# Mixing the tiles of the first feed-forward product among the seven products of the second in a fixed order, with the squares on the scalar engine

## The chip, the core and the metric

The kernel runs on one core of a Trainium2 chip. The metric is the device time of one launch in microseconds (us), less is better. Three runs of the kernel before gave 1634.02, 1637.30 and 1638.63 us.

## What is computed

A trunk of two layers over 512 latent tokens and 256 context tokens with 1024 features. Each layer has a group of mixers, an output projection, and then a squared-ReLU feed-forward block (4096 hidden features) with a gated residual and a layer norm. Layer 1 no longer needs the context's feed-forward. All of it is float32. What matters here:

```python
def channel_mlp(h, w1, w2):
    return jnp.square(jax.nn.relu(h @ w1)) @ w2
...
        f = channel_mlp(modulate(x, m[3], m[4]), w_ff1[l], w_ff2[l])
        x = layer_norm_affine(DN_ALPHA * x + m[5] * f, ln2_g[l], ln2_b[l])
```

In layer 0 the context goes through the same block with its own modulation and its own gate.

## The kernel before

**Products.** TensorE multiplies at reduced precision, so each float32 operand is split into a high half (a rounded copy, by the scalar engine) and a low half (the rest, a subtraction on the vector engine), and one product is three matmuls (`mm3`, line 135). A weight tile is a raw load into the pool `raw` of four rotating buffers (`pr`), then its two halves in the pool `W` (`load_w`, line 154; scalar engine line 162, vector engine line 165).

**The feed-forward block** is `ffn` (line 1181), called once per layer by `run`. N is 768 tokens in layer 0 (latent and context) and 512 in layer 1. The 4096 hidden features are 32 feature tiles of 128, f0 to f31, in eight chunks of four. A feature tile is 16 (layer 0: for latent and context separately) or 8 steps of three matmuls: 48 matmuls in layer 0, half of them 512 and half 256 columns wide, and 24 of 512 columns in layer 1. A relu (line 1199) takes it out of PSUM.

The second product of a chunk, squares of four feature tiles times 512 rows of w2, is done by the Strassen-Winograd scheme: tokens are halved (`half`), features are taken in pairs of tiles (two pairs per chunk), outputs are halved, and seven products with sums and differences of the blocks replace eight. Each product has HT row tiles (3 in layer 0, 2 in layer 1), and for each 6 matmuls of 512 columns: 18 or 12 matmuls per product. The parts:

- `operands` (line 1256): squares on GpSimd (line 1262), four sums per pair on GpSimd (line 1281), halves by the scalar engine (line 1274) and vector engine (line 1275), into tiles `fop`.
- `weights` (line 1295): four raw loads of w2, halves (lines 1307 and 1308), four differences on GpSimd (line 1312), which are written over the raw tiles.
- `ff2_chunk` (line 1327): the seven products; each result is added from PSUM into accumulators `acc` or the shared part `base` by the vector engine (line 1338). Between two products `more()` asks for the next operands.

The loop runs over chunks 0 to 6. A chunk's turn first builds the four feature tiles of the chunk after it (`ff1`), then its own seven products; the order on TensorE is left to the scheduler. The first chunk's tiles come from `ff1_first`, ahead of the loop. The last chunk, f28 to f31, has no Strassen products: its tiles are squared by `square` (line 1201) and go through an ordinary second product, `ff2_tile` (line 1373), 12 or 8 units of 12 matmuls behind everything else.

**The tail.** The gate rows are broadcast to 128 partitions by `rows2(0)` ahead of the loop (`bcast_rows`, line 1434: a DMA issued by the scalar engine in program order). Behind the loop each 128-row accumulator gets the shared part (vector engine, line 1418), is multiplied by the gate (GpSimd, line 1419) and gets the residual row `rawx` (vector engine, line 1420), which was loaded through the same four `raw` buffers (line 1414). Then come the rows ln2g and ln2b (`rows2(1)`), the four w2 tiles of the tail (`ff2_w`, line 1364), also through `raw`, the units with the gate applied (`fft`, line 1385, then an addition on GpSimd, line 1386), and the layer norm of each row tile.

Small pools that matter: `G`, four buffers (tag G), which hold `base`, the gates and the norm rows; PSUM: PA with three single banks, PF with one, P2 with two double banks.

Of the kernel before, what the change touches and what calls it, by code (L numbers as in the profile page):

```python
# [9 lines left out]
F32 = mybir.dt.float32  # L10
F32R = mybir.dt.float32r
AF = mybir.ActivationFunctionType
ALU = mybir.AluOpType
# [5 lines left out]
NL = 512  # L19
NC = 256  # L20
# [27 lines left out]
class Trunk:  # L48
# [102 lines left out]
                out=lo, in0=src, scalar=scale, in1=hi.bitcast(F32), op0=ALU.mult, op1=ALU.subtract  # L151
            )

    def load_w(self, pieces, shape, name, gate=None):

        nc = self.nc
        raw = self.pr.tile(shape, F32, name=self.nm("raw" + name), tag="raw")
        for sl, src in pieces:
            self.load(out=raw[sl], in_=src)
        hi = self.pw.tile(shape, F32R, name=self.nm("hi" + name), tag="W")  # L160
        lo = self.pw.tile(shape, F32R, name=self.nm("lo" + name), tag="W")
        i = nc.scalar.activation(out=hi, in_=raw, func=AF.Copy)  # L162
# [279 lines left out]
    def proj_T(self, l, hL, hC, c0, nf, evict, ctx_too, name):  # L442
# [738 lines left out]
    def ffn(self, l, hL, hC, x, xc, rows2, mod2, done):  # L1181
        nc, A = self.nc, self.A
        w1 = A["w_ff1"][l].rearrange("(k p) n -> p k n", p=128)
        w2 = A["w_ff2"][l].rearrange("(f p) n -> p f n", p=128)
        NCH = DFF // 512
        full = hC is not None

        def ff1_w(f):
            W = self.load_w([((slice(None),), w1[:, :, 128 * f:128 * f + 128])], [128, 8, 128], "w1",
                            self.gate if f < 8 else None)  # L1190
# [17 lines left out]
        N = NL + NC if full else NL  # L1208
        half = N // 2
        HT = half // 128  # L1210

        def ff1(c):
            rs = []
            for f in range(4 * c, 4 * c + 4):
                W = ff1_w(f)
                ps = self.P2("ff1")
                ff1_mm(ps[:, :NL], hL, 0, W)
                if full:
                    ff1_mm(ps[:, NL:NL + NC], hC, 0, W)
                r = self.T("relu", 768)  # L1220
                relu(r, 0, ps[:, :N])
                rs.append(r)
            return rs

        def ff1_first():

# [26 lines left out]
                            relu(rs[f - 1 + i], NL, big[:, 512 * i:512 * i + 256])  # L1253
            return rs

        def operands(rs):

            pool = nc.gpsimd  # L1260
            for r in rs:
                pool.tensor_tensor(out=r[:, :N], in0=r[:, :N], in1=r[:, :N], op=ALU.mult)  # L1262
            q = []
            for p in range(2):
                tmp = self.T("fsum", 768)
                e, o = rs[2 * p], rs[2 * p + 1]
                q.append((e[:, :half], o[:, :half], e[:, half:N], o[:, half:N], tmp[:, :half], tmp[:, half:N]))

            def halves(k):
                res = []  # L1270
                for v in q:
                    z = self.Z("fop")
                    hi, lo = z[:, :half], z[:, half:N]
                    nc.scalar.activation(out=hi, in_=v[k], func=AF.Copy)  # L1274
                    nc.vector.tensor_tensor(out=lo, in0=v[k], in1=hi.bitcast(F32), op=ALU.subtract)  # L1275
                    res.append((hi, lo))
                return res

            def sums(o, a, b, op):
                for v in q:  # L1280
                    pool.tensor_tensor(out=v[o], in0=v[a], in1=v[b], op=op)

            yield halves(0)
            sums(4, 2, 3, ALU.add)
            yield halves(4)
            sums(5, 4, 0, ALU.subtract)
            yield halves(5)
            sums(4, 1, 5, ALU.subtract)
            yield halves(4)
            sums(2, 0, 2, ALU.subtract)  # L1290
            yield halves(2)
            yield halves(1)
            yield halves(3)

        def weights(c):

            pool = nc.gpsimd
# [12 lines left out]

            def diff(o, a, b):
                pool.tensor_tensor(out=o, in0=a, in1=b, op=ALU.subtract)  # L1312

            b11, b12, b22, b21 = raw(0, 0), raw(0, 1), raw(1, 1), raw(1, 0)
            yield halves(b11)
            diff(b11, b12, b11)
            yield halves(b11)
            diff(b11, b22, b11)
            yield halves(b11)
            diff(b12, b22, b12)  # L1320
            yield halves(b22)
            yield halves(b12)
            yield halves(b21)
            diff(b21, b21, b11)
            yield halves(b21)

        def ff2_chunk(c, left, acc, base, more):


            B = weights(c)  # L1330
            seen = set()

            def add(ps, key, sl):
                if c == 0 and key not in seen:
                    seen.add(key)
                    nc.scalar.activation(out=sl, in_=ps, func=AF.Copy)
                else:
                    nc.vector.tensor_tensor(out=sl, in0=ps, in1=sl, op=ALU.add)  # L1338

            for i, to in enumerate((("11", "B"), ("12", "22"), ("B",), ("12",), ("21", "22"), ("11",), ("21",))):  # L1340
                if i % 2 == 0:
                    banks = [self.PA("ff2") for _ in range(HT)]
                else:
                    big = self.P2("ff2")
                    banks = [big[:, 0:512], big[:, 512:1024]]
                    if HT > 2:
                        banks.append(self.PF("ff2") if i == 3 else self.P2("ff2")[:, 0:512])
                W, a = next(B), left[i]
                for t in range(HT):
                    for p in range(2):  # L1350
                        self.mm3(
                            banks[t], [h[:, 128 * t:128 * t + 128] for h in a[p]],
                            [h[:, p, :] for h in W], p == 0, p == 1,
                        )
                    for q in to:
                        if q == "B":
                            sl = base[t]
                        else:
                            n = int(q[1]) - 1
                            sl = acc[HT * (int(q[0]) - 1) + t][:, 512 * n:512 * n + 512]  # L1360
                        add(banks[t], (q, t), sl)
                more()

        def ff2_w(c, n):
            return [
# [22 lines left out]
        rs = ff1_first()  # L1388
        big = [self.G([128, 1024], "base") for _ in range((HT + 1) // 2)]
        base = [big[t // 2][:, 512 * (t % 2):512 * (t % 2) + 512] for t in range(HT)]  # L1390
        gl, gc = rows2(0)

        xr = self.pd.tile([N, D], F32, name=self.nm("xr"), tag=self.nm("xr"))
        for j, t in enumerate(x + (xc or [])):
            nc.sync.dma_start(out=xr[128 * j:128 * j + 128, :], in_=t)
        acc = [self.X([128, 1024], "acc") for _ in range(N // 128)]
        left = list(operands(rs))
        for c in range(NCH - 1):
            nxt, ops = [], None
            if c < NCH - 2:  # L1400
                ops = operands(ff1(c + 1))
                nxt += [next(ops), next(ops)]

            def more():
                if ops is not None:
                    nxt.extend([z for z in [next(ops, None)] if z is not None])

            ff2_chunk(c, left, acc, base, more)
# [256 lines left out]
```

## Time and profile before

| what | us |
|---|---|
| median of three runs | 1637.3 |
| lowest, highest | 1634.02, 1638.63 |
| profiled execution, its own time | 1640.47 |
| span of its trace | 1638.4 |
| TensorE busy | 1484.5 (91%) |
| vector engine busy | 1102.6 (67%) |
| scalar engine busy | 661.7 (40%) |
| GpSimd busy | 600.9 (37%) |

The profile is of one execution. PE is TensorE's matmul, PEld its weight load, DVE the vector engine, ACT the scalar engine, POOL is GpSimd, SP issues most loads; ACTq and SPq are DMA issues. Times in the views are us from the start of the span. PEclk is the mean granted clock of TensorE, 1.00 for 2.4 GHz and 0.50 for 1.2 GHz.

### The profile page before, as it was taken

To read this page: it belongs to the slowest core of one execution; us is meant where nothing else is said; L and a number is where in the kernel's file an instruction comes from. 1 tells how busy PE (TensorE), PEld (TensorE's weight loads), DVE (VectorE), ACT (ScalarE), POOL (GpSimd) and SP (SyncE) were. 2 spreads that over 40 slices of the span, in tenths; PEclk is the share of its full clock that TensorE was granted. 3 is DMA by queue.
4 is the path that set the end of the run, shared out by engine and by line. 5 is a ranking of instruction groups with operands and counts; after the bars stand their busy time and mean duration, and the time that the engine had idled before them with its cause. 6 is when DMAs were issued, how large, how long until landed. Compare 5 with 4: busy or idle time off the path is not lost. (4 is left out here: it accounts for less than half of the span.)

```text
span 1638.4 us, 23881 instructions
## 1 busy us (share of the span) xinstructions
PE 1484.5 (91%) x9228; PEld 1226.5 (75%) x9228; DVE 1102.6 (67%) x1811; ACT 661.7 (40%) x1207; POOL 600.9 (37%) x478
## 2 busy tenths in 40 slices
PE   5899889999999899999997989989989999898895
PEld 3689667787988687787876767867778778777674
DVE  3384655566574847648399589575465877678896
ACT  3433455425562323323221355355436643334331
POOL 1021333233363252432525151143242655443633
PEclk9999899999999999999999889999998999999997
DMA  8442366265212302123014423245265122233152
GB/s 287 142 117 63 122 217 193 80 223 179 78 39 65 98 29 80 39 64 91 28 62 128 130 78 116 65 149 162 86 217 179 52 89 91 81 100 103 52 154 77
DMA packets 150954, 180.45 MB, mean 110 GB/s; under 512 B 9096, under 2 KB 96568, under 8 KB 150840
## 3 DMA queue, kind: packets, MB, share of 16 engines
q1 hardware_dynamic: 140792, 160.42, 31.3%
q10 hardware_dynamic: 10048, 18.49, 3.4%
q8 instruction: 73, 1.20, 0.3%
q14 instruction: 41, 0.34, 0.1%
HBM read 169.43 MB, written 9.46 MB: 109 GB/s over the span
## 5 line engine op out<-in xcount | busy, mean ns | idle before, releaser
L133 PE MATMUL ff<-hiw,fop 128*128 128x512 f32 x980 | 325.0, 406 | 36.3 <-DVE acc L1338 35.6
L133 PEld LDWEIGHTS ff<-hiw,fop 128*128 128x128 f32 x980 | 191.3, 195 | 87.9 <-DVE acc L1338 25.3
L133 PE MATMUL ff<-hh,hiw 128*128 128x512 f32 (+1 forms) x672 | 241.6, 360 | 13.6 <-DVE acc L1338 9.5
L1308 DVE TENSOR_TENSOR low<-raww,hiw 128x1024 fp32r<-128x1024 f32 x98 | 136.7, 1397 | 159.7 <-ACT hiw L1307 159.4
L133 PE MATMUL ff<-hl,hiw 128*128 128x512 f32 (+1 forms) x672 | 240.4, 358 | 0.0
L133 PE MATMUL ff<-hh,low 128*128 128x512 f32 (+1 forms) x672 | 239.4, 356 | 0.7 <-DVE low L165 0.7
L1262 POOL TENSOR_TENSOR relu<-relu 128x768 f32<-128x768 f32 (+1 forms) x56 | 91.2, 1631 | 318.3 <-ACT relu L1199 318.3
L133 PE MATMUL ff<-low,fop 128*128 128x512 f32 x490 | 199.2, 406 | 6.7 <-DVE low L1308 6.7
L1307 ACT ACTIVATE hiw<-raww 128x1024 fp32r<-128x1024 f32 x98 | 103.2, 1060 | 231.6 <-PE ff L133 157.7
L1338 DVE TENSOR_TENSOR acc<-ff,acc 128x512 f32<-128x512 f32 x260 | 167.9, 676 | 12.3 <-PE ff L133 12.2
L1312 POOL TENSOR_TENSOR raww<-raww,raww 128x1024 f32<-128x1024 f32 x56 | 137.3, 2452 | 86.7 <-DVE low L1308 67.5
L133 PEld LDWEIGHTS ff<-hh,hiw 128*128 128x128 f32 x672 | 128.8, 192 | 36.0 <-issue 13.6
L133 PEld LDWEIGHTS ff<-hh,low 128*128 128x128 f32 x672 | 128.0, 190 | 19.2 <-DVE low L165 1.1
L133 PEld LDWEIGHTS ff<-hl,hiw 128*128 128x128 f32 x672 | 128.8, 192 | 18.0
L162 ACT ACTIVATE hiw<-raww 128x1024 fp32r<-128x1024 f32 x64 | 66.5, 1057 | 143.0 <-PE ff L133 103.2
L133 PEld LDWEIGHTS ff<-low,fop 128*128 128x128 f32 x490 | 95.5, 195 | 32.1 <-DVE low L1308 13.0
L547 POOL TENSOR_SCALAR p<-p,rec 128x768 f32<-128x768 f32 (+3 forms) x80 | 63.4, 796 | 143.1 <-DVE rec L546 133.4
L1275 DVE TENSOR_TENSOR fop<-relu,fop 128x384 fp32r<-128x384 f32 (+1 forms) x112 | 87.0, 801 | 39.9 <-ACT fop L1274 39.9
L165 DVE TENSOR_TENSOR low<-raww,hiw 128x1024 fp32r<-128x1024 f32 x64 | 82.0, 1289 | 14.6 <-ACT hiw L162 14.5
L133 PE MATMUL ada<-wada,sc 128*32 128x128 f32 x1536 | 62.4, 300 | 22.5 <-DMA wada<-in_w_ada 22.5
L1275 DVE TENSOR_TENSOR fop<-fsum,fop 128x384 fp32r<-128x384 f32 (+1 forms) x84 | 75.0, 914 | 7.3 <-ACT fop L1274 7.3
L1274 ACT ACTIVATE fop<-relu 128x384 fp32r<-128x384 f32 (+1 forms) x112 | 50.2, 466 | 68.1 <-POOL relu L1262 34.3
(362 smaller groups left out, 3237.7 us busy)
## 6 DMA issues: line engine op xcount, KB each, us to landing
raww<-in_w_ff SPq DMA_DIRECT2D x120, 512.0 KB, 4.2
wada<-in_w_ada SPq DMA_DIRECT2D x96, 512.0 KB, 4.6
rawwo<-in_w_out SPq DMA_DIRECT2D x16, 512.0 KB, 7.7
rawx<-xr SPq DMA_DIRECT2D x10, 512.0 KB, 3.4
rawz<-in_w_ff SPq DMA_DIRECT2D x8, 512.0 KB, 4.6
xr<-x SPq DMA_DIRECT2D x8, 512.0 KB, 5.1
rawwb<-in_w_in SPq DMA_DIRECT2D x12, 256.0 KB, 4.3
gate<-grow ACTq DMA_DIRECT2D x6, 512.0 KB, 7.2
```

The source lines that it names most:

```text
L133: return self.pinned(self.nc.tensor.matmul(out, lhsT, rhs, start=start, stop=stop))
L162: i = nc.scalar.activation(out=hi, in_=raw, func=AF.Copy)
L165: nc.vector.tensor_tensor(out=lo, in0=raw, in1=hi.bitcast(F32), op=ALU.subtract)
L547: nc.gpsimd.tensor_scalar(out=p[:, :keep], in0=p[:, :keep], scalar1=rec, scalar2=1.0, op0=ALU.mult, op1=ALU.mult)
L1262: pool.tensor_tensor(out=r[:, :N], in0=r[:, :N], in1=r[:, :N], op=ALU.mult)
L1274: nc.scalar.activation(out=hi, in_=v[k], func=AF.Copy)
L1275: nc.vector.tensor_tensor(out=lo, in0=v[k], in1=hi.bitcast(F32), op=ALU.subtract)
L1307: nc.scalar.activation(out=hi, in_=t, func=AF.Copy)
L1308: nc.vector.tensor_tensor(out=lo, in0=t, in1=hi.bitcast(F32), op=ALU.subtract)
L1312: pool.tensor_tensor(out=o, in0=a, in1=b, op=ALU.subtract)
L1338: nc.vector.tensor_tensor(out=sl, in0=ps, in1=sl, op=ALU.add)
```

## The change

Four things, all in `ffn`:

1. TensorE's instructions are chained in the order of the program within the loop (`self.pin = True`; `mm` then makes each matmul follow the one before), and that order is a string per chunk: f is a feature tile of the chunk after, a digit a product. "f01f23f45f6" for chunks 0 to 5, "01f23f456ff" for chunk 6, whose four tiles are f28 to f31.
2. Operands are made per pair, as soon as its two tiles are there; their squares are done by the scalar engine. The products come in another order with other targets, the differences of weights are rearranged accordingly (four per chunk, as before), and the accumulators' first writes (copies by the scalar engine) are kept over chunks in `seen`.
3. The raw loads of w1 within the loop go through the pool `G` (`spare=True`) instead of `raw`.
4. The gate rows, `rows2(0)`, are loaded behind the loop.

```diff
-    def load_w(self, pieces, shape, name, gate=None):
+    def load_w(self, pieces, shape, name, gate=None, spare=False):
...
-        raw = self.pr.tile(shape, F32, name=self.nm("raw" + name), tag="raw")
+        raw = self.G(shape, "raw" + name) if spare else self.pr.tile(
+            shape, F32, name=self.nm("raw" + name), tag="raw")
...
-        def operands(rs):
+        def operands(e, o):
...
-            for r in rs:
-                pool.tensor_tensor(out=r[:, :N], in0=r[:, :N], in1=r[:, :N], op=ALU.mult)
+            for r in (e, o):
+                nc.scalar.activation(out=r[:, :N], in_=r[:, :N], func=AF.Square)
+            tmp = self.T("fsum", 768)
+            a11, a12, a21, a22 = e[:, :half], o[:, :half], e[:, half:N], o[:, half:N]
+            s1, s2 = tmp[:, :half], tmp[:, half:N]
...
+            z11 = halves(a11)
+            pool.tensor_tensor(out=s1, in0=a21, in1=a22, op=ALU.add)
+            pool.tensor_tensor(out=s2, in0=s1, in1=a11, op=ALU.subtract)
+            pool.tensor_tensor(out=a21, in0=a11, in1=a21, op=ALU.subtract)
+            pool.tensor_tensor(out=a11, in0=a12, in1=s2, op=ALU.subtract)
+            return [z11] + [halves(v) for v in (a11, a12, s1, s2, a21, a22)]
...
-            b11, b12, b22, b21 = raw(0, 0), raw(0, 1), raw(1, 1), raw(1, 0)
+            b11, b22, b21, b12 = raw(0, 0), raw(1, 1), raw(1, 0), raw(0, 1)
             yield halves(b11)
...
+            diff(b12, b12, b11)
+            yield halves(b22)
+            diff(b22, b22, b12)
             diff(b11, b22, b11)
...
+            diff(b21, b21, b22)
+            for t in (b12, b22, b11, b21):
+                yield halves(t)
+
+        TO = (("11", "B"), ("12",), ("11",), ("12", "22"), ("B",), ("21", "22"), ("21",))
+
+        def product(i, B, left, acc, base, seen):
...
-        gl, gc = rows2(0)
...
-        left = list(operands(rs))
+        left = [operands(rs[2 * p], rs[2 * p + 1]) for p in range(2)]
+        seen = set()
+        self.pin = True
         for c in range(NCH - 1):
-            nxt, ops = [], None
-            if c < NCH - 2:
-                ops = operands(ff1(c + 1))
-                nxt += [next(ops), next(ops)]
...
+            B = weights(c)
+            rs, nxt = [], []
+            order = "f01f23f45f6" if c < NCH - 2 else "01f23f456ff"
+            for o in order:
+                if o != "f":
+                    product(int(o), B, left, acc, base, seen)
+                    continue
+                rs.append(ff1_tile(4 * c + 4 + len(rs), True))
+                if c < NCH - 2 and len(rs) % 2 == 0:
+                    nxt.append(operands(*rs[-2:]))
             left = nxt
-
-        rs = ff1(NCH - 1)
+        self.pin = None
+
+        gl, gc = rows2(0)
```

TensorE in a chunk of layer 0, before. Each row is the first matmul of a group with one output; `ff` tiles fed by `hh` are feature tiles (48 matmuls each), those fed by `fop` are row tiles of products.

```order
L133 MATMUL ff_1249_5934<-hiw_1251_5936,fop_5393 128x512
...
L133 MATMUL ff_1261_5996<-hh_4127,hiw_1259_5992 128x512
...
L133 MATMUL ff_1266_6053<-hh_4127,hiw_1264_6049 128x512
...
L133 MATMUL ff_1271_6110<-hh_4127,hiw_1269_6106 128x512
...
L133 MATMUL ff_1276_6167<-hh_4127,hiw_1274_6163 128x512
...
L133 MATMUL ff_1284_6238<-hiw_1291_6249,fop_5726 128x512
...
L133 MATMUL ff_1295_6285<-hiw_1297_6288,fop_5734 128x512
...
L133 MATMUL ff_1309_6362<-hiw_1310_6364,fop_5820 128x512
```

The same place now:

```order
L133 MATMUL ff_1259_5992<-hh_4127,hiw_1257_5988 128x512
...
L133 MATMUL ff_1261_6043<-hiw_1268_6054,fop_5672 128x512
...
L133 MATMUL ff_1270_6082<-hiw_1272_6085,fop_5679 128x512
...
L133 MATMUL ff_1277_6116<-hh_4127,hiw_1275_6112 128x512
...
L133 MATMUL ff_1287_6195<-hiw_1290_6200,fop_5682 128x512
...
L133 MATMUL ff_1292_6225<-hiw_1294_6228,fop_5685 128x512
...
L133 MATMUL ff_1299_6262<-hh_4127,hiw_1297_6258 128x512
...
L133 MATMUL ff_1301_6313<-hiw_1304_6316,fop_5688 128x512
```

Four feature tiles stood together, then all seven products; now a tile, two products, a tile, two products, and so on.

GpSimd in a chunk of layer 1 now; rows of `raww` are weight differences, rows of `fsum` and `relu` are the operand sums (the second output into `relu` is the left operand of product 1):

```order
L1295 TENSOR_TENSOR raww_2671_13315<-raww_2671_13315,raww_2668_13309 128x1024
L1274 TENSOR_TENSOR fsum_13228<-relu_13150,relu_13224 128x256
L1295 TENSOR_TENSOR raww_2669_13311<-raww_2669_13311,raww_2671_13315 128x1024
L1275 TENSOR_TENSOR fsum_13228<-fsum_13228,relu_13150 128x256
L1276 TENSOR_TENSOR relu_13150<-relu_13150 128x256
L1295 TENSOR_TENSOR raww_2668_13309<-raww_2669_13311,raww_2668_13309 128x1024
L1277 TENSOR_TENSOR relu_13150<-relu_13224,fsum_13228 128x256
L1295 TENSOR_TENSOR raww_2670_13313<-raww_2670_13313,raww_2669_13311 128x1024
```

The sums of one pair and the four weight differences stand in turn; the squares that stood here are gone.

The scalar engine at the end of layer 0's loop now (`gate` are the moved loads):

```order
L1204 ACTIVATE fh_8471<-relu_8361 128x768
L1200 ACTIVATE relu_8418<-ff_1598_8369 128x768
L1416 DMA gate_8420<-grow_4403 128x1024
L1416 DMA gate_8422<-grow_4405 128x1024
L1416 DMA ln2g_8457<-in_ln_g 128x1024
L1416 DMA ln2b_8459<-in_ln_b 128x1024
L1204 ACTIVATE fh_8476<-relu_8418 128x768
L163 ACTIVATE hiw_1619_8483<-raww_1618_8481 128x1024
```

Before, the two gate loads stood among the first relus ahead of the loop, and only ln2g and ln2b here. SP still has the six `rawx` loads ahead of the tail's four weight loads.

## Rows read from the trace of the kernel before

**Rows 1.** Busy time of each engine over the whole execution (page, part 1).

```profile
PE 1484.5 (91%) x9228; PEld 1226.5 (75%) x9228; DVE 1102.6 (67%) x1811; ACT 661.7 (40%) x1207; POOL 600.9 (37%) x478
```

**Rows 2.** Busy time by stretch: layer 0's loop, its tiles, its products.

```profile
core 0: us, PE busy (x) PEld busy (x) DVE busy (x) ACT busy (x) POOL busy (x), PEclk, DMA share, GB/s
436.76:921.42 484.66, 453.39 (x2229) 378.29 (x2228) 327.26 (x390) 153.64 (x221) 200.71 (x117) 0.97 0.23 68
638.14:671.55 33.41, 33.41 (x192) 29.59 (x193) 8.32 (x7) 6.81 (x9) 15.88 (x9) 1.00 0.10 32
671.55:706.79 35.24, 31.49 (x129) 24.49 (x127) 34.06 (x49) 14.02 (x21) 10.38 (x7) 0.95 0.32 90
```

**Rows 3.** The same, layer 1's loop, its first two tiles, a steady chunk.

```profile
1266.13:1595.66 329.53, 303.53 (x1263) 242.65 (x1262) 262.37 (x316) 134.81 (x212) 171.51 (x113) 0.96 0.30 92
1266.13:1277.04 10.91, 10.91 (x51) 9.02 (x49) 6.90 (x7) 5.66 (x15) 9.67 (x10) 1.00 0.24 88
1418.27:1465.31 47.04, 42.97 (x182) 34.69 (x181) 35.90 (x45) 19.10 (x30) 23.49 (x17) 0.96 0.29 90
```

**Rows 4.** Waits of TensorE in 430 to 870 us (total, times, longest).

```profile
PE ff L133 <- DVE acc L1338: 18.3, 23, 2.1
```

**Rows 5.** Waits of TensorE in 1290 to 1600 us.

```profile
PE ff L133 <- DVE acc L1338: 21.2, 9, 3.7
```

**Rows 6.** Timeline, layer 1's loop end: start, us, engine, line, operation.

```profile
1580.73 1.21 DVE L1420 TENSOR_TENSOR acc<-acc,rawx 128x1024 f32<-128x1024 f32 x1
...
1587.25 1.06 ACT L162 ACTIVATE hiw<-raww 128x1024 fp32r<-128x1024 f32 x1 [6.61 <-DMA raww<-in_w_ff]
1588.21 0.58 ACT L1199 ACTIVATE relu<-ff 128x512 f32<-128x512 f32 x1
1588.83 0.63 ACT L1203 ACTIVATE fh<-relu 128x512 fp32r<-128x512 f32 x1
...
1591.07 1.22 DVE L165 TENSOR_TENSOR low<-raww,hiw 128x1024 fp32r<-128x1024 f32 x1
```

**Rows 7.** GpSimd by line in 1418.27 to 1465.31: busy us, mean ns, idle before.

```profile
L1312 POOL TENSOR_TENSOR raww<-raww,raww 128x1024 f32<-128x1024 f32 x5 | 12.1, 2418 | 3.5 <-DVE low L1308 3.4
L1262 POOL TENSOR_TENSOR relu<-relu 128x512 f32<-128x512 f32 x4 | 6.3, 1564 | 18.5 <-ACT relu L1199 18.5
L1281 POOL TENSOR_TENSOR relu<-relu 128x256 f32<-128x256 f32 x2 | 2.6, 1318 | 0.0
...
L1281 POOL TENSOR_TENSOR fsum<-relu,relu 128x256 f32<-128x256 f32 x2 | 1.5, 734 | 0.1
```

**Rows 8.** Timeline of the scalar engine: issues of the row broadcasts.

```profile
327.43 1.21 ACTq L1437 DMA_DIRECT2D gate<-grow  x2
...
437.02 0.33 ACTq L1437 DMA_DIRECT2D gate<-grow  x1
...
921.47 0.34 ACTq L1437 DMA_DIRECT2D ln2g<-in_ln_g  x1
```

**Rows 9.** Timeline of GpSimd, multiplications by the gate, layer 0.

```profile
879.20 9.44 POOL L1419 TENSOR_TENSOR acc<-acc,gate 128x1024 f32<-128x1024 f32 x3 [5.89 <-DVE acc L1338]
889.27 6.12 POOL L1419 TENSOR_TENSOR acc<-acc,gate 128x1024 f32<-128x1024 f32 x2 [0.62 <-DVE acc L1418]
```

**Rows 10.** Timeline of the vector engine, residual additions, layer 0.

```profile
889.72 9.03 DVE L1420 TENSOR_TENSOR acc<-acc,rawx 128x1024 f32<-128x1024 f32 x4
```

**Rows 11.** Timeline of SP's issues, layer 0's loop end.

```profile
869.87 23.61 SPq L116 DMA_DIRECT2D rawx<-xr  x6
896.50 6.47 SPq L116 DMA_DIRECT2D raww<-in_w_ff  x4
```

**Rows 12.** The gate tiles' loads, all six.

```profile
DMA to landing us min/median/max: 4.1/7.2/10.2
```

**Rows 13.** Busy time by stretch, the tails (columns as in rows 2).

```profile
921.42:958.93 37.51, 34.86 (x145) 27.70 (x143) 29.57 (x49) 9.60 (x18) 18.75 (x15) 0.95 0.28 91
1595.66:1623.41 27.75, 25.69 (x96) 19.39 (x95) 19.17 (x32) 6.68 (x10) 11.41 (x10) 0.88 0.19 64
```

More of the change, by code (lines that the diff above doesn't have):

```diff
@@ L1186, in ffn, with ff1_w @@
         full = hC is not None
-        def ff1_w(f):
+        def ff1_w(f, spare=False):
             W = self.load_w([((slice(None),), w1[:, :, 128 * f:128 * f + 128])], [128, 8, 128], "w1",
-                            self.gate if f < 8 else None)
+                            self.gate if f < 8 else None, spare)
             return [[W[j][:, k, :] for j in range(2)] for k in range(KT)]
@@ L1210, in ffn, with ff1_tile @@
         HT = half // 128
[L1212 to L1223, printed above, removed]
+        def ff1_tile(f, spare):
+            W = ff1_w(f, spare)
+            ps = self.P2("ff1")
+            ff1_mm(ps[:, :NL], hL, 0, W)
+            if full:
+                ff1_mm(ps[:, NL:NL + NC], hC, 0, W)
+            r = self.T("relu", 768)
+            relu(r, 0, ps[:, :N])
+            return r
         def ff1_first():
@@ L1254, in ff1_first @@
             return rs
-        def operands(rs):
+        def operands(e, o):
             pool = nc.gpsimd
-            for r in rs:
-                pool.tensor_tensor(out=r[:, :N], in0=r[:, :N], in1=r[:, :N], op=ALU.mult)
[L1263 to L1293, printed above, removed]
@@ new lines, in operands, with halves @@
+            for r in (e, o):
[3 more added lines that the diff above has]
+            s1, s2 = tmp[:, :half], tmp[:, half:N]
+            def halves(v):
+                z = self.Z("fop")
+                hi, lo = z[:, :half], z[:, half:N]
+                nc.scalar.activation(out=hi, in_=v, func=AF.Copy)
+                nc.vector.tensor_tensor(out=lo, in0=v, in1=hi.bitcast(F32), op=ALU.subtract)
+                return hi, lo
@@ L1295, in weights @@
+            z11 = halves(a11)
[4 more added lines that the diff above has]
+            return [z11] + [halves(v) for v in (a11, a12, s1, s2, a21, a22)]
         def weights(c):
-            pool = nc.gpsimd
             def raw(odd, n):
@@ L1311, in diff @@
             def diff(o, a, b):
-                pool.tensor_tensor(out=o, in0=a, in1=b, op=ALU.subtract)
-            b11, b12, b22, b21 = raw(0, 0), raw(0, 1), raw(1, 1), raw(1, 0)
+                nc.gpsimd.tensor_tensor(out=o, in0=a, in1=b, op=ALU.subtract)
+            b11, b22, b21, b12 = raw(0, 0), raw(1, 1), raw(1, 0), raw(0, 1)
             yield halves(b11)
-            diff(b11, b12, b11)
-            yield halves(b11)
+            diff(b12, b12, b11)
+            yield halves(b22)
+            diff(b22, b22, b12)
@@ L1318, in weights @@
             diff(b11, b22, b11)
[L1319 to L1322, printed above, removed]
             yield halves(b21)
[L1324 to L1362, printed above, removed]
@@ new lines, in weights @@
+            diff(b21, b21, b22)
[3 more added lines that the diff above has]
+        def product(i, B, left, acc, base, seen):
+            if i in (0, 2, 4, 6):
+                banks = [self.PA("ff2") for _ in range(HT)]
+            else:
+                big = self.P2("ff2")
+                banks = [big[:, 0:512], big[:, 512:1024]]
+                if HT > 2:
+                    banks.append(self.PF("ff2"))
+            W = next(B)
+            for t in range(HT):
+                ps = banks[t]
+                for p in range(2):
+                    self.mm3(
+                        ps, [h[:, 128 * t:128 * t + 128] for h in left[p][i]],
+                        [h[:, p, :] for h in W], p == 0, p == 1,
+                    )
+                for q in TO[i]:
+                    if q == "B":
+                        sl = base[t]
+                    else:
+                        n = int(q[1]) - 1
+                        sl = acc[HT * (int(q[0]) - 1) + t][:, 512 * n:512 * n + 512]
+                    if (q, t) in seen:
+                        nc.vector.tensor_tensor(out=sl, in0=ps, in1=sl, op=ALU.add)
+                    else:
+                        seen.add((q, t))
+                        nc.scalar.activation(out=sl, in_=ps, func=AF.Copy)
@@ L1396, in ffn @@
         acc = [self.X([128, 1024], "acc") for _ in range(N // 128)]
-        left = list(operands(rs))
+        left = [operands(rs[2 * p], rs[2 * p + 1]) for p in range(2)]
+        seen = set()
+        self.pin = True
         for c in range(NCH - 1):
-            nxt, ops = [], None
-            if c < NCH - 2:
-                ops = operands(ff1(c + 1))
-                nxt += [next(ops), next(ops)]
[L1404 to L1408, printed above, removed]
+            B = weights(c)
[8 more added lines that the diff above has]
+                    nxt.append(operands(*rs[-2:]))
             left = nxt
-        rs = ff1(NCH - 1)
+        self.pin = None
+        gl, gc = rows2(0)
         for j, t in enumerate(acc):
```

## The prediction

> **What bounds the kernel now.** I read the page's busy table first: TensorE is busy 91% of the span [rows 1], so a reordering can only win what TensorE loses in gaps and at the lower clock. The view of stretches then shows where it loses. In layer 0 the loop runs from the first tile behind the opening to the end of the last feature tile, 484.66 us, with TensorE busy 453.39 and a mean granted clock of 0.97 [rows 2]. Its four feature tiles of one chunk take 33.41 us for 192 matmuls with no gap at all; the seven products behind them take 35.24 us with 31.49 busy and a clock of 0.95 [rows 2]. In layer 1 the loop takes 329.53 us with 303.53 busy, a steady chunk 47.04 with 42.97 [rows 3].
>
> What would the loops take without loss? In layer 1 the first two tiles, 48 matmuls of 512 columns, take 10.91 us at full clock [rows 3] (the row counts 51 records that touch the stretch), so one takes 10.91/48 = 0.2273 us. A chunk of layer 0 is 33.41 us of tiles and 7 x 18 = 126 product matmuls, 28.64 us: 62.05, and seven of them 434.3. The loop takes 484.66, so **50.3 us are lost**. A chunk of layer 1 is 96 + 84 matmuls, 40.91 us, seven 286.4, of 329.53: **43.1 us lost**. Together 93.4.
>
> The view of waits names the loss: in 430 to 870 us TensorE's product matmuls wait 18.3 us in 23 waits for the vector engine's evictions (line 1338) [rows 4]; in layer 1 21.2 us in 9 waits for the evictions, up to 3.7 at once [rows 5]. The rest of the 93 is clock: 0.95 over 35.24 us costs 1.76 us per chunk, and the clock falls in the stretch with the waits, not in the tiles. The reason is in the vector engine's load: it is busy 8.32 of the 33.41 us of tiles and 34.06 of the 35.24 us of products [rows 2]. It idles through one half and is full in the other. Over a whole chunk it is not full: in layer 1 35.90 of 47.04 us [rows 3]. Averaged over a chunk without gaps that is 35.90/40.91 = 88%.
>
> **The change part by part.**
>
> *The mixed order.* All matmuls stay; now no more than two products stand between two tiles (before: seven together). A layer-0 pair of products (2 x 18 matmuls, 8.2 us) is followed by a tile (33.41/4 = 8.35 us), in which its evictions can finish. So the vector engine's 88% in layer 1, and less in layer 0 (42.39 us by the row of tiles plus products, 8.32 + 34.06, of 62.05, 68%), is spread evenly, and most of the 93.4 us goes. What is late next is the operand chain of product 1. Its left operand for the second pair needs the last tile's relu, square, four sums on GpSimd (the fourth is the operand), a copy and a low half. From that tile's end until product 1 TensorE has product 6, a tile and product 0. In layer 1 that is 12 + 24 + 12 = 48 matmuls, 10.9 us. The chain is 0.58 + 0.63 (relu and square, [rows 6]), 4 sums of 0.73 to 1.32, about 4.0 [rows 7], some 1.1 for copy and low half: 6.7, and with the two weight differences of 2.42 [rows 7] that stand among the sums in the new GpSimd order 11.6. So it is 4 us early if the differences pass before it, 0.7 late if both fall in it. In layer 0 the time is 18 + 18 matmuls and a tile, 16.5 us, and the sums are longer by half, about 13.5 with both differences: no wait. I keep a residue of 0.5 us per chunk in layer 0 (4 in all) and 1.1 in layer 1 (8 in all; waits of 0.7 with some clock). Its bounds are 0, and 3.5 per chunk, where the whole gain is gone (below). **Loops: 93.4 - 12 = -81 us.**
>
> *Squares on the scalar engine.* 56 of 1.6 to 1.8 us leave GpSimd [rows 7]. On ScalarE the nearest row is the tail's square, 0.63 us for 512 columns [rows 6], four per chunk: 2.5 us on an engine that is busy 19.10 of 47.04 [rows 3]. That costs nothing as long as it stays half idle; without this cover it would be those 2.5 us a chunk. GpSimd's 6.3 us per chunk go, which is what brings the chain above to 11.6 rather than later.
>
> *First-product weights through another pool; operands per pair; targets and weight order changed.* Same bytes and the same instructions, but for the squares; nothing on the path.
>
> *The gate loads behind the loop.* This is the cost. Before, the two gate broadcasts of layer 0 were issued from 437.02 us on [rows 8] and had landed long before use: by the end of the last tile (E, 921.42) the last multiplications by the gate (889.27 + 6.12) and most residual additions (four in 889.72 + 9.03) were done [rows 9, 10], and so the weights of the last second-product tiles, which rotate through the same four buffers as the six residual rows, were issued from 896.50 on [rows 11]. Now the scalar engine issues the gates only after the last relu; the ln2g load in the same place of the old program went out at 921.47, E + 0.05 [rows 8]. A gate takes 4.1 us to land at best, 7.2 in the median, 10.2 at worst [rows 12]; with nothing else loading I take 4.1. Then, in layer 0: three multiplications at 9.44/3 = 3.15 [rows 9], the third residual addition 1.21 [rows 6], which frees the buffer that the first of the four weight loads needs. From the end of such an addition to the start of the weight's first half was 1587.25 - (1580.73 + 1.21) = 5.3 us in layer 1, where the load waited for just that; half 1.06, low half 1.22 [rows 6]. Sum: E + 0.05 + 4.1 + 9.45 + 1.21 + 5.3 + 1.06 + 1.22 = **E + 22.4**. Each further weight tile follows a further multiplication, 3.15 apart: the fourth at E + 31.8. Behind it stand ten of the twelve units, 27 to 31 us (5/6 of the tail's 34.86 busy us [rows 13] is 29), so TensorE ends at E + 62 to 66, where it was 37.5 [rows 13]: +24 to +28, **I take 26**. In layer 1 there are only four residual rows for four buffers, so the first weight waits for the first addition alone: E + 0.05 + 4.1 + 3.15 + 1.21 + 5.3 + 2.28 = E + 16.1, the fourth at E + 25.5, six of eight units behind it (3/4 of 25.69 is 19.3): E + 44 to 48 against 27.75 [rows 13]: **+18**. Bounds for both tails: 38 (first values of both ranges, units overlapping better) and 56 (TensorE has idled, so the restart runs partly at the lower of the two levels, 1.2 instead of 2.4 GHz: the tail of layer 1 ran at 0.88 after its small gaps [rows 13], 12% of 50 us is 6, twice).
>
> The Trainium skill, page "DMA: Bandwidth & Descriptors", section "Rules for kernel authors", says to issue a load early and to wait late; this part of the change does the opposite, and the rows above are its price, 44 us against none.
>
> *Sum:* 1640.5 (the profiled execution) - 81 + 44 = 1603. The profiled execution stands 3.2 us above the median of the runs, so by the median **1600 us**. Its own range, with the residue from 0 to 1.8 per chunk in both layers and the tails from 38 to 56: 1582 to 1625.
>
> **Rivals.**
>
> *The operand chain takes the place of the eviction wait (slower).* Before product 1 TensorE waits in every chunk, since the weight differences on GpSimd themselves wait (3.4 us for the low half that reads the same buffer [rows 7]) and hold the sums behind them, in order. One difference and one sum are 2.42 + 0.74 = 3.2 us of wait, and the clock takes 1.76 more as it does now: 5 us per chunk, 70 over fourteen. The gain is then 23 and the tails cost 44: +21, **1658**. It decides from (93.4 - 44)/14 = 3.5 us per chunk. For it: the vector engine's 88% and the order of GpSimd. Against it: 3 to 4 us of slack in layer 0. Chance 0.12.
>
> *The tail is hidden.* If the first weight tile doesn't stand behind the residual rows, or half the work fits below what waits, the 44 go: 1640.5 - 81 - 3 = **1556**. Against it: the order of SP has all residual rows ahead of the four weights, through four buffers. Chance 0.08.
>
> *The gates land late.* Four broadcasts of 512 KB (two gates, ln2g, ln2b) are now issued in one go. Where two gates were issued together with ln1g and ln1b, at 327.43 [rows 8], and beside loads of x, one took up to 10.2 us [rows 12]; this adds 6.1 per layer, **1612**. The same skill page, section "Issuing engines are not separate DMA queues", says that transfers of all issuing engines run on the same 16 DMA engines and interleave. By that rule the first gate lands with the others; the trace agrees in the 10.2, but the same row has 4.1 for the two issued at 437.02 [rows 8]. Chance 0.10, inside the main range.
>
> *The change doesn't do what it says:* excluded as far as the order shows; TensorE's order is the alternating one.
>
> **How the numbers follow.** The forecast as worked out has 0.70, late gates 0.10, the chain 0.12, a hidden tail 0.08. The range 1570 to 1640 leaves out the last two. A measurement of this kernel tells about 0.3% (4.9 us) from no change: between 1632 and 1642 lie only a residue near 3.5 per chunk or both bounds at their worst, 0.05. Faster 0.83, same 0.05, slower 0.12.
>
> **What would show it.** The loop of layer 0 at about 438 us and of layer 1 at about 295, clock at 0.99 or above in both, and TensorE's waits for evictions nearly gone. Behind each loop a hole of 15 to 22 us on TensorE, with the gate's landing, GpSimd's multiplications by the gate and the residual additions in it, and tails of about 63 and 46 us. I am wrong if loops keep more than 3 us a chunk (then the waits name GpSimd or the operand copies before product 1), or if the weights of the tail are loaded before E + 10.

## The result, and the profile after

The change made the kernel slower: 1786.18 us median of four runs (1777.12 to 1788.38) against 1636.32 for the kernel before, ratio 1.0905 with a 95% interval of 1.0863 to 1.0947. I had predicted 1600. The profiled execution took 1784.67 us with a span of 1782.9.

TensorE does the same matmuls and is busy a little longer, but for a smaller share of the span. The busy table of the page after, answering to [rows 1]:

```profile
PE 1518.9 (85%) x9228; PEld 1251.1 (70%) x9228; DVE 1064.2 (60%) x1811; ACT 696.4 (39%) x1263; POOL 506.2 (28%) x422
```

The view of stretches after, answering to [rows 2, 3, 13] (same columns): both loops, a steady chunk of each layer, then for each layer the hole behind the last feature tile and the tail's matmuls.

```profile
434.36:959.43 525.07, 468.50 (x2228) 390.64 (x2226) 282.56 (x382) 170.83 (x244) 127.80 (x81) 0.94 0.18 54
1333.62:1724.50 390.88, 322.80 (x1262) 253.54 (x1260) 235.78 (x313) 146.24 (x238) 116.64 (x81) 0.91 0.23 70
652.78:728.15 75.37, 67.64 (x319) 56.39 (x318) 40.40 (x55) 23.76 (x34) 19.44 (x13) 0.93 0.20 56
959.43:981.06 21.63, 0.01 (x2) 0.00 (x1) 16.61 (x7) 2.71 (x3) 17.13 (x6) 0.62 0.49 170
981.06:1020.92 39.86, 36.30 (x146) 28.73 (x146) 34.00 (x54) 12.61 (x20) 18.95 (x16) 0.91 0.41 134
1724.50:1739.44 14.94, 0.00 (x2) 0.00 (x1) 9.57 (x5) 2.28 (x3) 10.56 (x4) 0.66 0.45 143
1739.44:1766.94 27.50, 25.03 (x96) 19.22 (x96) 20.38 (x29) 6.21 (x7) 11.14 (x10) 0.88 0.23 75
1446.58:1500.58 54.00, 44.43 (x182) 35.10 (x181) 34.55 (x46) 20.67 (x34) 17.97 (x13) 0.94 0.26 78
```

The loops, which were to shrink by 81 us, grew: 525.07 against 484.66 and 390.88 against 329.53, +101.8 together. What follows the last tile takes 21.63 + 39.86 = 61.5 us against 37.51, and 14.94 + 27.50 = 42.4 against 27.75: +38.7. That is 140.5 of the 144.5 us between the spans.

The vector engine is less busy than before in both loops, and yet TensorE waits for it more. Waits of TensorE after, in 430 to 1060 and in 1300 to 1783, answering to [rows 4, 5]:

```profile
PE ff L133 <- DVE acc L1336: 50.4, 19, 3.9
PE ff L133 <- ACT hiw L163: 22.3, 2, 21.6
...
PE ff L133 <- DVE acc L1336: 47.2, 19, 3.4
PE ff L133 <- ACT hiw L163: 14.9, 1, 14.9
PE ff L133 <- DVE fop L1270: 10.2, 7, 2.6
```

19 waits for evictions per loop, three in each chunk but the first: one in each of products 1, 3 and 5. The timelines of TensorE and of the vector engine around product 1 of a layer-0 chunk show where (the first word behind the two times is the engine; in brackets stands the idle time before and what ended it):

```profile
666.11 0.39 PE L133 MATMUL ff<-low,fop 128*128 128x512 f32 x1
666.34 0.39 PE L133 MATMUL ff<-hiw,fop 128*128 128x512 f32 x1
669.84 0.50 PE L133 MATMUL ff<-hiw,fop 128*128 128x512 f32 x1 [3.12 <-DVE acc L1336]
...
666.77 1.22 DVE L1291 TENSOR_TENSOR low<-raww,hiw 128x1024 fp32r<-128x1024 f32 x1
667.90 0.69 DVE L1336 TENSOR_TENSOR acc<-ff,acc 128x512 f32<-128x512 f32 x1
668.50 0.68 DVE L1336 TENSOR_TENSOR base<-ff,base 128x512 f32<-128x512 f32 x1
669.10 0.68 DVE L1336 TENSOR_TENSOR acc<-ff,acc 128x512 f32<-128x512 f32 x1
```

Product 0 ends near 665.2 and product 1 begins without a wait. It stops after six matmuls, one row tile, and goes on when the eviction of just that row tile has ended (669.10 + 0.68 = 669.78). The vector engine reached it only at 669.10, behind a weight's low half and the last two evictions of product 0. But the second row tile goes into another bank: `big[:, 512:1024]`. Products 1, 3 and 5 keep their first two row tiles in the two halves of one double PSUM tile (`P2`), and the program writes the eviction of the first half between the matmuls of the two halves. My theory (A) after reading this: the wait is for the tile, not for the bank, so each row tile's eviction stands between the matmuls; a fixed TensorE order lets nothing pass. The kernel before had the same code, but the scheduler put other matmuls into the gaps. The evictions of its layer-0 chunk show it: product 1 adds each row tile to two parts of `acc`, product 2 adds to `base`, and the last two additions of product 1 (688.55) stand behind all three of product 2:

```profile
679.93 2.47 DVE L1338 TENSOR_TENSOR acc<-ff,acc 128x512 f32<-128x512 f32 x4
...
684.55 0.68 DVE L1338 TENSOR_TENSOR base<-ff,base 128x512 f32<-128x512 f32 x1
685.15 0.67 DVE L1338 TENSOR_TENSOR acc<-ff,acc 128x512 f32<-128x512 f32 x1
685.75 0.67 DVE L1338 TENSOR_TENSOR base<-ff,base 128x512 f32<-128x512 f32 x1
...
686.82 0.67 DVE L1338 TENSOR_TENSOR base<-ff,base 128x512 f32<-128x512 f32 x1
...
688.55 1.27 DVE L1338 TENSOR_TENSOR acc<-ff,acc 128x512 f32<-128x512 f32 x2
```

Rival B: the vector engine is simply late with evictions, and a wait removed here returns elsewhere. Rival C: the mixture itself brings operands late.

### The profile page after: what moved, and what is told of

The parts are those of the page before. It is cut to its first block, busy times and chain, and to the rows that moved or that the text cites. A ratio compares the mean times of both kernels' runs of the same rounds, so it can differ in the third digit from the quotient of the medians.

```text
span 1782.9 us, 23916 instructions
## 1 busy us (share of the span) xinstructions
PE 1518.9 (85%) x9228; PEld 1251.1 (70%) x9228; DVE 1064.2 (60%) x1811; ACT 696.4 (39%) x1263; POOL 506.2 (28%) x422
## 5 line engine op out<-in xcount | busy, mean ns | idle before, releaser
L133 PE MATMUL ff<-hiw,fop 128*128 128x512 f32 x980 | 357.6, 431 | 124.6 <-DVE acc L1336 97.6
L133 PEld LDWEIGHTS ff<-hiw,fop 128*128 128x128 f32 x980 | 202.9, 207 | 191.5 <-DVE acc L1336 113.1
L1291 DVE TENSOR_TENSOR low<-raww,hiw 128x1024 fp32r<-128x1024 f32 x98 | 136.2, 1392 | 223.9 <-ACT hiw L1290 223.9
L1290 ACT ACTIVATE hiw<-raww 128x1024 fp32r<-128x1024 f32 x98 | 103.6, 1060 | 327.9 <-PE ff L133 327.8
L1336 DVE TENSOR_TENSOR acc<-ff,acc 128x512 f32<-128x512 f32 x260 | 172.1, 684 | 76.1 <-PE ff L133 73.2
L133 PE MATMUL ff<-low,fop 128*128 128x512 f32 x490 | 208.2, 425 | 0.0
L133 PEld LDWEIGHTS ff<-low,fop 128*128 128x128 f32 x490 | 102.1, 208 | 19.4
L166 DVE TENSOR_TENSOR low<-raww,hiw 128x1024 fp32r<-128x1024 f32 x64 | 91.4, 1429 | 36.4 <-ACT hiw L163 36.4
L1270 DVE TENSOR_TENSOR fop<-relu,fop 128x384 fp32r<-128x384 f32 (+1 forms) x140 | 76.0, 573 | 54.1 <-ACT fop L1269 54.1
L1269 ACT ACTIVATE fop<-relu 128x384 fp32r<-128x384 f32 (+1 forms) x140 | 58.2, 460 | 80.3 <-POOL relu L1277 79.8
L1274 POOL TENSOR_TENSOR fsum<-relu,relu 128x384 f32<-128x384 f32 (+1 forms) x28 | 25.7, 917 | 217.7 <-ACT relu L1261 217.7
L1200 ACT ACTIVATE relu<-ff 128x768 f32<-128x768 f32 (+2 forms) x76 | 45.5, 606 | 71.1 <-PE ff L133 70.7
```

Source lines behind the costliest of these rows:

```text
L133: return self.pinned(self.nc.tensor.matmul(out, lhsT, rhs, start=start, stop=stop))
L1269: nc.scalar.activation(out=hi, in_=v, func=AF.Copy)
L1270: nc.vector.tensor_tensor(out=lo, in0=v, in1=hi.bitcast(F32), op=ALU.subtract)
L1274: pool.tensor_tensor(out=s1, in0=a21, in1=a22, op=ALU.add)
```

## The experiments

The stages of each run, in us from its trace: the loop (first matmul behind the opening to the end of the last feature tile) and what follows up to the end of the tail's matmuls.

| run | layer 0: loop, behind | layer 1: loop, behind | median |
|---|---|---|---|
| kernel before | 484.7, 37.5 | 329.5, 27.7 | 1637.3 |
| the change | 525.1, 61.5 | 390.9, 42.4 | 1786.2 |
| e1_evict_behind | 439.1, 60.7 | 314.1, 42.5 | 1621.9 |
| e2_before_evict_behind | 450.8, 37.5 | 324.9, 30.5 | 1597.0 |
| e3_free_order | 436.5, 60.8 | 302.9, 42.7 | 1608.6 |
| e4_gates_before_last_tiles | 521.1, 40.4 | 391.6, 28.0 | 1740.2 |
| e5_behind_and_gates | 437.5, 46.9 | 315.4, 33.1 | 1602.2 |
| e6_free_and_gates | 441.9, 41.8 | 306.0, 29.4 | 1581.1 |
| e7_squares_alone | 484.2, 37.5 | 325.1, 26.5 | 1635.1 |
| e8_squares_back | 445.8, 62.8 | 339.8, 42.7 | 1656.1 |
| e9_free_behind_gates | 438.4, 47.3 | 291.8, 33.4 | 1576.6 |
| e11_one_product_behind | 489.6, 60.4 | 361.2, 41.9 | 1719.3 |
| e12_best_weights_first | 438.4, 46.7 | 292.5, 32.7 | 1573.1 |
| e13_late_gates_weights_first | 439.2, 53.4 | 314.3, 24.4 | 1600.1 |

e3, e4 and e11 were each run once.

**Evictions behind both banks (e1).** In `product`, where `mms(t)` holds the six matmuls of row tile t:

```diff
-            for t in range(HT):
-                ps = banks[t]
...
+            odd = i % 2 == 1
+            for t in range(HT):
+                ps = banks[t]
+                if not odd or t > 1:
+                    mms(t)
+                elif t == 0:
+                    mms(0)
+                    mms(1)
```

> The changed kernel, but in products 1, 3 and 5 the matmuls of both banks of the double PSUM tile come before the evictions of either. Theory A (the second bank's first matmul is made to wait for the eviction of the first bank, because both are one tile, and TensorE's fixed order lets nothing pass): the three waits per chunk of layer 0 (3.12, 2.58, 2.02 us) and the three of layer 1 (2.98, 2.60, 2.03) go, and the lower clock behind each; a chunk of layer 0 falls from 75.4 to 62 to 65 us, of layer 1 from 54 to 43 to 47 (the operand waits of 2 us stay); the tails keep their holes; time 1615 to 1655. Rival B (the vector engine is too late with its evictions, whichever bank): the waits move to the next product that needs the bank, chunks stay above 71 and 51, time above 1740.

Measured 1621.85 (1620.73 to 1622.62), ratio to the kernel before 0.9916 (0.9892 to 0.9939): 164 us less than the change, by moving instructions only. The stretches of its loops:

```profile
435.95:875.10 439.15, 436.33 (x2228) 373.04 (x2226) 282.80 (x382) 170.11 (x244) 128.28 (x81) 1.00 0.20 64
1248.13:1562.25 314.12, 296.06 (x1262) 239.42 (x1260) 238.82 (x313) 145.33 (x238) 118.93 (x81) 0.98 0.28 88
```

The vector engine is as busy as in the change (282.80 against 282.56), evictions included; no wait for an eviction is left in either loop, and layer 0's clock is 1.00. B falls. What is left in layer 1 are waits for operands, in the view of waits from 1200 to 1730:

```profile
PE ff L133 <- ACT fop L1269: 8.6, 6, 5.9
PE ff L133 <- DVE fop L1270: 7.6, 6, 1.4
```

**One product only (e11).** As e1 with `odd = i == 1`.

> The changed kernel (1786.2) with the evictions behind both banks in product 1 alone, not in 3 and 5. Theory A: the cost goes by places; one of three waits per chunk goes in each layer, those of products 3 and 5 stay at 2.6 and 2.0 us; product 1's are the longest, so 35 to 50% of the 164 us that all three gave: 1704 to 1729. Rival B (evictions late as a whole): the waits of 3 and 5 grow by what product 1 gives up, above 1755.

Measured 1719.28, 66.9 us less, 41% of the 164. In its timeline product 1 has no wait, and the others keep theirs to within 0.01 us (layer 0, one chunk):

```profile
676.38 0.50 PE L133 MATMUL ff<-hiw,fop 128*128 128x512 f32 x1 [2.58 <-DVE acc L1345]
695.22 0.50 PE L133 MATMUL ff<-hiw,fop 128*128 128x512 f32 x1 [2.03 <-DVE acc L1345]
```

The cost goes by places, as A says.

**The same edit on the kernel before (e2).**

> The kernel before with the same edit. Theory A: the same dependence made the eviction waits of the kernel before (18.3 us in 430 to 870, 21.2 in 1290 to 1600), where the scheduler's order filled part of each with matmuls of other products; without it the waits go and part of the clock comes back: 1585 to 1620. Rival B: those waits were of a full vector engine, 1630 to 1645.

Measured 1596.97 (1596.56 to 1600.69), ratio 0.9771 (0.9742 to 0.9801). The loop of layer 0 falls from 484.7 to 450.8 with a clock of 1.00, that of layer 1 by 4.6 us only. So two thirds of the 50.3 us that I had read as an uneven vector engine in layer 0 were this dependence. Waits for evictions, in 432 to 870 and in 1200 to 1730 us, are down to these,

```profile
PE ff L133 <- DVE acc L1338: 10.4, 7, 1.8
...
PE ff L133 <- DVE acc L1338: 11.3, 9, 2.8
```

from 18.3 and 21.2. But in layer 1 the clock of the loop is no better (0.95, where it was 0.96):

```profile
1224.14:1549.02 324.88, 307.07 (x1263) 245.30 (x1261) 263.62 (x313) 130.08 (x210) 172.50 (x113) 0.95 0.29 91
```

So for most of layer 1's 43.1 us this run leaves rival B open.

**Free order (e3).** `self.pin = True` is left out.

> The changed kernel with TensorE's order left to the scheduler (self.pin stays None), all else as in the change. Theory A: the scheduler moves other matmuls into the waits for the first bank's eviction, the eviction waits in the loop of layer 0 fall below half of 50 us; the tails stay: 1650 to 1730. Rival C (the mixture itself is wrong, its operands come late): the time stays above 1760.

Measured 1608.55, below what I expected, C falls. TensorE's order now alternates within the product: in a chunk of layer 0 twelve matmuls of an odd product (its first row tile and its third, which has a bank of its own), some 23 to 26 of the feature tile, the odd product's last six (the second half of the double tile), then the rest of the feature tile. No wait for evictions by the vector engine is left in 437 to 873:

```profile
PE ff L133 <- ACT acc L1339: 1.9, 1, 1.9
PE ff L133 <- ACT hiw L1290: 0.2, 1, 0.2
```

The loop of layer 0 takes 436.5 us, against the 434.3 without loss of the prediction. The mixture is good; the fixed order, with nothing to fill the wait for the tile, made the loss in the loops.

**The gates (e4).** In the last chunk, ahead of the third tile, and with f30 and f31 through the raw pool:

```diff
+                last = c == NCH - 2 and len(rs) >= 2
+                if last and len(rs) == 2:
+                    gl, gc = rows2(0)
+                rs.append(ff1_tile(4 * c + 4 + len(rs), not last))
...
-        gl, gc = rows2(0)
```

> The changed kernel, but the gate rows are loaded before the last two feature tiles, whose weights go through the raw pool again. The tails' theory: the holes of 21.6 and 14.9 us behind the loops shrink to under 8 and 6, time 1740 to 1760, the loops unchanged. Rival: the residual rows and the weights of the tail still queue for the four raw buffers behind the multiplications on GpSimd, which can't start before the last products: holes above 15 and 10, time above 1770.

Measured 1740.23. The loops stayed within 4 us, the time behind them fell by 21.1 and 14.4 us, 35.5 of the 46 us that this run gained. So the late gates cost about the 44 us that they were forecast to.

**Both (e5), and gates in the free order (e6).**

> The fixed mixed order with evictions behind both banks (as e1_evict_behind, 1621.9) and the gate rows before the last two feature tiles (as e4). If the two losses are separate they add: the gates gave 1786 - 1740 = 46 beside the slow loop, and take 21.7 + 14.7 us of holes here; 1575 to 1592. If the tail's work only moves to another queue (GpSimd's multiplications behind the last products): 1600 or more.

> The mixed program with TensorE's order free (as e3, 1608.6) and the gate rows before the last two feature tiles. Losses separate: 1608.6 - 40 = 1560 to 1575. If the scheduler puts the last tiles elsewhere once the gates stand between them: 1585 or more.

Measured 1602.15 (1599.76 to 1604.53) and 1581.12 (1579.51 to 1584.86; ratio 0.966, 0.963 to 0.9689). Both gain less than forecast, 20 and 27 us instead of about 40. The holes are gone, but the tails behind stay longer than the 37.5 of before: 46.9 and 41.8 in layer 0. In e4 the slow loop gave GpSimd time to multiply by the gate before the last tile ended (done at 952.55, in e5 only at 882.27). The tail's weights in SP's issues, first e4, whose last tile ends at 955.93, then e5, where that is at 876.71:

```profile
938.03 16.01 SPq L116 DMA_DIRECT2D raww<-in_w_ff  x4
```

```profile
869.82 15.07 SPq L116 DMA_DIRECT2D raww<-in_w_ff  x4
```

18 us ahead of the end there, 7 us here. The two losses do not add; the faster the loop, the more of the tail's preparation stands behind it.

**Squares alone (e7) and squares back (e8).** e7 is the kernel before with `nc.scalar.activation(..., func=AF.Square)` for the squares; e8 is e1 with them on GpSimd again.

> The kernel before with nothing changed but the squares on the scalar engine. Theory A: they are on no path, 1628 to 1645. Rival: GpSimd's time (1.6 to 1.8 us, 56 times) stood before the operand sums and its end lets the operands come earlier: below 1625; or the scalar engine's copies of weights fall behind them: above 1650.

> As e1_evict_behind (1621.9), but the squares go back to GpSimd. Theory: in layer 1 the operand chain before product 1 gets longer by 1.56 - 0.63 = 0.9 us, and by up to 2 squares where they queue, so its waits of 2.0 us per chunk grow to 3 to 5: 1628 to 1645; in layer 0 the chain keeps its slack and the loop stays at 439. Rival: no effect (within 1617 to 1627), as the weight differences set the chain.

e7: 1635.08 (1631.48 to 1638.18), ratio 0.9983 (0.9966 to 0.9999), hardly a difference. e8: 1656.13 (1654.32 to 1658.20), 34 us above e1 (33 by the two ratios to the kernel before, 1.0115 and 0.9916), more than expected. Its waits for operands in 1190 to 1600:

```profile
PE ff L133 <- ACT fop L1269: 24.4, 7, 7.0
PE ff L133 <- DVE fop L1270: 10.6, 5, 2.4
```

and GpSimd's timeline of one chunk of layer 1 shows the squares (line 1261) queued among weight differences and sums:

```profile
1350.64 1.59 POOL L1261 TENSOR_TENSOR relu<-relu 128x512 f32<-128x512 f32 x1 [4.13 <-ACT relu L1200]
1352.19 2.39 POOL L1295 TENSOR_TENSOR raww<-raww,raww 128x1024 f32<-128x1024 f32 x1
1354.55 1.72 POOL L1274 TENSOR_TENSOR fsum<-relu,relu 128x256 f32<-128x256 f32 x1
1356.23 2.40 POOL L1295 TENSOR_TENSOR raww<-raww,raww 128x1024 f32<-128x1024 f32 x1
1358.58 1.72 POOL L1275 TENSOR_TENSOR fsum<-fsum,relu 128x256 f32<-128x256 f32 x1
1360.26 0.74 POOL L1276 TENSOR_TENSOR relu<-relu 128x256 f32<-128x256 f32 x1
1360.96 1.04 POOL L1261 TENSOR_TENSOR relu<-relu 128x512 f32<-128x512 f32 x1
1361.96 0.72 POOL L1277 TENSOR_TENSOR relu<-relu,fsum 128x256 f32<-128x256 f32 x1
```

From the start of the second square to the operand of product 1 are 12.0 us, more than the 10.9 us of matmuls that TensorE has in the meantime. So the same edit is worth almost nothing in the old order, where a chunk's operands were made beside the products of the chunk before, and 34 us in the mixed one.

**Towards a better kernel (e9, e12, e13).** e9 is e6 with e1's edit. e12 is e9, and e13 is e1, with the four weight tiles of the tail (`Ws`) loaded ahead of the residual rows.

> As e6_free_and_gates (1581.1: free order, gate rows before the last two tiles), with the evictions of products 1, 3 and 5 behind both banks as well. Theory A: the free order had already filled the waits for the first bank, so little is left to win: 1572 to 1586. Rival: the split groups of matmuls still cost something in the free order, or the scheduler's order gets worse without the dependence: below 1570 or above 1588.

> As e9_free_behind_gates (1576.6), with the four weight tiles of the tail loaded ahead of the residual rows. Tail theory: the weights no longer stand behind the multiplications by the gate, so the stretch behind the last tile falls from 47.3 and 33.4 us to 38 to 42 and 28 to 31: 1562 to 1573. Rival: then the residual additions, which the tail's own additions need, come too late and the row tiles end later: 1575 or more.

> As e1_evict_behind (1621.9; gates still behind the loop), with the four weight tiles of the tail loaded ahead of the residual rows. Tail theory (it was the queue through four buffers that let a late gate hold TensorE, not the gate itself): the holes of 21.7 and 14.7 us on TensorE go below 4, the stretch behind the last tile falls from 60.7 and 42.5 to 42 to 50 and 32 to 38: 1590 to 1608. Rival: the gate holds the tail anyway, since each unit's eviction (fft) and addition need it: above 1612.

e9: 1576.64 (1569.87 to 1578.10), ratio 0.9616 (0.9585 to 0.9646), as expected hardly better than e6. e12: 1573.06 (1571.30 to 1574.80), ratio 0.9605 (0.9588 to 0.9622): **4% under the kernel before**, like e9, from which the intervals don't tell it apart; its tail is hardly shorter (46.7 and 32.7), so the theory's forecast for it failed. TensorE now waits for something else in the same place, the low half of the squared tile (`fl`), made by the vector engine; from 870 to 940 of e12:

```profile
PE ff L133 <- DVE fl L1206: 10.9, 1, 10.9
```

e13: 1600.07 (1594.33 to 1603.20), within what was expected, but for another reason in each layer. In layer 1 the stretch behind the loop falls from 42.5 to 24.4 us, below the 27.7 of the kernel before; its first units now start 5.8 us ahead of the last tile's end. So there the queue through the four buffers was the whole cost. In layer 0 it falls by 7 us only: TensorE starts the units, and then waits 15.3 us for the vector engine's multiplication by the gate (`fft`):

```profile
PE ff L133 <- DVE fft L1371: 15.3, 1, 15.3
```

Both the theory and its rival hold, one in each layer.

## Why the prediction was wrong

**The step that failed: "spread evenly, and most of the 93.4 us goes", with a residue of 0.5 and 1.1 us per chunk.** I read the waits for evictions (line 1338, [rows 4, 5]) as an overfull vector engine in the product half, from its 34.06 of 35.24 us [rows 2]. I never asked which matmul waited for which eviction. It was the second half of a double tile for the first half, a wait that spreading the vector engine's load does not remove and that comes back in each odd product: 3.12, 2.58 and 2.02 us per chunk in layer 0. The free order had covered most of it with matmuls of other products, as the evictions of the kernel before show, and I did not ask what those were for. Pinning the order took the cover away: I costed that at nothing. e1, e3, e11 and e2 show it from four sides.

The reading was not wrong everywhere. In layer 1 the dependence alone gave 4.6 of 43.1 us (e2), and e9, which has the rest of the change as well, in a free order and with the gates ahead of the last two tiles, has loops 12.4 and 33.1 us shorter than e2. Which part of it gives that, the spread evictions or another, no run separates.

**The size.** A steady chunk of layer 0 took 75.37 us against 62.05 without loss, 13.3 over: 7.72 in the three waits, the other 5.6 as longer busy time of TensorE (67.64 against 62.05), nearly all in matmuls at the lower level of the clock, 1.2 GHz (0.93 in the stretch, 7% of 75.37 is 5.3).

**Loops without that dependence: right in kind.** I forecast about 438 and 295 us; e1 has 439.1 and 314.1, e9 438.4 and 291.8. In layer 1 of e1 the loss is in the place I named, product 1's operand, but 27.7 us (314.1 - 286.4) instead of 8. TensorE idles 18.1 us of it (314.12 - 296.06), the rest is clock. A wait of 2.0 us per chunk, not 0.7: both differences of 2.40 fall among the sums, and two of the four sums took 1.7 us where the others took 0.7. And in the last chunk products 0 and 1 stand first, with no tile ahead of them, which I had not reckoned: there the wait is 5.9 us. The two long sums of a chunk of e1:

```profile
1338.35 1.72 POOL L1275 TENSOR_TENSOR fsum<-fsum,relu 128x256 f32<-128x256 f32 x1
...
1343.08 1.73 POOL L1277 TENSOR_TENSOR relu<-relu,fsum 128x256 f32<-128x256 f32 x1
```

**The squares "cost nothing": right, but they are worth something.** In the mixed order they are worth 34 us (e8). The Trainium skill, page "Perfetto Trace Analysis", section "Optimizing GPSIMD Operations", advises to use other engines than GpSimd where one can; e8 against e1 agrees with 34 us, e7 with under 6.

**The gate loads: right.** Forecast: first weight ready at E + 22.4 and E + 16.1 (E is the end of the last feature tile), tails +26 and +18. Measured: holes of 21.6 and 14.9 us, tails +24.0 and +14.7. The timeline of layer 0's end shows the chain as it was added up (E is 959.43):

```profile
959.48 0.82 ACTq L1416 DMA_DIRECT2D gate<-grow  x2
...
963.93 17.82 POOL L1398 TENSOR_TENSOR acc<-acc,gate 128x1024 f32<-128x1024 f32 x6 [78.90 <-DMA gate<-grow]
...
976.29 8.07 SPq L116 DMA_DIRECT2D raww<-in_w_ff  x4
...
979.95 1.06 ACT L163 ACTIVATE hiw<-raww 128x1024 fp32r<-128x1024 f32 x1 [17.80 <-DMA raww<-in_w_ff]
```

The first gate landed 4.4 us after its issue, though four broadcasts went out together; that rival's 10.2 did not come.

**The rivals.** The slower one named a wait before product 1 and was worth 1658. It took the right side by the wrong mechanism; but for one wait in the last chunk, that wait exists in layer 1 only.

**Sums.** Three are off, and none decides. The terms of product 1's chain add up to 6.3 and 11.1 us, not 6.7 and 11.6, so by them it is 0.2 us late at worst. The fourth weight at E + 31.8 with 27 to 31 us behind it ends at E + 59 to 63, not 62 to 66 (measured: E + 61.5). And TensorE's idle time in both loops was 57 us (484.66 - 453.39 and 329.53 - 303.53), so the clock's part of the 93.4 us was 36, where I put down to it all but the 39.5 of waits for evictions.

Not tried: the mixed order with the gates ahead of the loop as before. The four raw buffers hold a chunk's four w2 blocks until product 6, so w1 needs the pool G in between, and in layer 0 base and gates would fill it. That the wait is for the tile is shown by moving evictions; a version with three single PSUM tiles per odd product was not run either.

## What to carry to other kernels

Before fixing an engine's order, list what each wait in the trace waits for, matmul by matmul: a free order can cover waits that the data do not ask for, and a fixed one then pays them in full. If two banks share one tile, write both banks' matmuls ahead of either's eviction, or give each its own tile. And a load that is moved to a later place can come onto the path, although its data are needed late, if its consumers free the buffers of what is loaded next.

## What the runs showed of the hardware

Banks that are tiles of their own cost no wait here: in product 0 the evictions from 663.44 on ran while TensorE filled the next banks without a gap. The Trainium skill, page "PSUM — Partial Sum Buffer", section "PSUM bank collisions raise a hardware error", says that only accesses to the same bank (in the same quarter of partitions) have to be kept apart; this trace agrees for such separate tiles (no wait in products 0, 2, 4 and 6 for their own evictions), and no run here reads one half of the double tile while the other is written.

Short waits are dear: three waits of 2 to 3 us per chunk brought the granted clock of a loop from 1.00 (e1) to 0.94, so that 7.7 us of waits cost 13.3.
